# Every fourth weight piece: the low half by a ScalarE negation and an accumulating transfer instead of a VectorE subtraction

## The chip, the cores and the metric

The kernel runs on one core of one Trainium2 chip. The metric is the device time of one execution in microseconds. Before the change three runs took 945.02, 945.37 and 944.0 us, so the median is 945.02 us.

## The reference

Two layers of a hybrid encoder over 256 frames of width 2048. Each layer multiplies the frames by one wide input matrix, runs three groups of heads on the result (band attention, gated linear attention, attention into 256 memory frames), multiplies each group by a SiLU gate, and maps the concatenation back by an output matrix, with a residual and a layer norm. Cut to its matrix products:

```python
def hybrid_layer(x, mem, w_in, rel_table, gate_w, gate_b, gla_norm_g, w_mem_kv, w_out, ln_g, ln_b):
    h = x @ w_in                       # (256, 2048) @ (2048, 6672), split into a_q, a_k, a_v, a_z, b_*, m_*
    ...
    mkv = mem @ w_mem_kv               # (256, 2048) @ (2048, 1024)
    ...
    y = jnp.concatenate([y_a * jax.nn.silu(a_z), y_b * jax.nn.silu(b_z), y_m * jax.nn.silu(m_z)], axis=-1)
    out = y @ w_out                    # (256, 2048) @ (2048, 2048)
    return layer_norm(DEEPNORM_ALPHA * x + out, ln_g, ln_b)
```

All of it is float32. What takes the time are these products with weights: some 170 MB of weights are read once and each is used for 256 frames.

## The kernel before

**Products in two halves.** TensorE's fast 32-bit type (fp32r) holds fewer digits than float32. So each float32 operand is split into a high part (the value rounded to fp32r) and a low part (the value minus its high part, again fp32r), and a product is the sum of three: high by high, low by high, high by low. The helper `parts(hi, lo, src)` makes both parts: ScalarE copies `src` to `hi`, rounding it (L117), and VectorE subtracts `hi` from `src` into `lo` (L118).

**Pieces.** The weights come in pieces of 128 partitions x 1024 values (512 KB; those of the value projection 128 x 776, 388 KB). The helper `piece(src, n, kp)` (its transfer is at L140 or L138) takes three buffers, `raw`, `wh` and `wl`, from a pool `wp` with four buffers for each of the three names; SyncE's queue transfers the weights into `raw`, and `parts` makes `wh` and `wl`. TensorE then uses the piece at once: 16 matmuls in the groups that hold the weights still (`ws_half`), 12 in the groups that hold the frames still (`as_group`). A buffer comes free when its last reader is done. So the copy into `wh` of a piece waits for TensorE to be done with the piece four earlier, and its raw transfer waits until the subtraction of the piece four earlier has read `raw`.

**Order of the groups.** In each layer: memory values (`G_MV`, 8 pieces), memory keys (`G_MK`, 8), the gated heads' q and k (`G_BQK`, 8), values (32 of the narrower pieces, in four groups), q and k of the attention heads (32), memory q (8), four gate groups (32), and the output matrix (32, of which the last 8 each come as two transfers, because their source is a list). In layer 0 the first four pieces of all are made by another helper, `begin_pieces`. While a group runs, the heads' own small work (matmuls into tiles called `bk`) is mixed in between its pieces by `tick()`. From the last two gate groups to the end of the output matrix nothing is mixed in.

**What sets the order.** TensorE's and SyncE's instructions are issued in the order of the program. Those of VectorE, ScalarE and GpSimd are placed by a scheduler that simulates the kernel when it is built; `piece` runs at high priority. Each engine then works through its own list strictly in order, and an instruction that waits holds up all behind it.

**GpSimd** has little to do before the change: it starts the small transfers (gate weights, layer norm rows `ln_g` and `ln_b`, L707 and L708), clears a few tiles, and does six multiplications and additions of the layer norm between the layers (L515 and L516).

Lines of the kernel are given as in the program before the change; the change adds eight lines within and above `piece`, so that behind it L515 becomes L523.

## Time and profile before

| what | value |
|---|---|
| median of 3 runs | 945.02 us |
| the profiled execution's own time | 944.11 us |
| its span, first to last instruction | 942.3 us |
| time outside the span | 1.8 us |
| TensorE busy, share of the span | 98% |
| VectorE busy | 62% |
| ScalarE busy | 53% |
| GpSimd busy | 3% |
| mean granted TensorE clock | 0.994 |
| mean rate of transfers | 190 GB/s |

In the profile PE is TensorE's matmul side and PEld its weight loads, DVE is VectorE, ACT ScalarE, POOL GpSimd and SP SyncE. A busy TensorE is a modelled quantity, since matmuls overlap; whether it is truly at its pace is read from how evenly the pieces follow each other. A row of the timeline gives the start and the length in microseconds, the engine, the line, the operation with output and inputs, the shapes, and in brackets how long the engine sat idle before it and what ended that. "us to landing" is the time from the issue of a transfer until its data is there.

### The profile page before, as it was taken

Reading aid. Unit: us, or ns where it says so; the run is one execution under the profiler, and the core shown is the slowest. Engines: PE = TensorE matmul, PEld = TensorE weight load, DVE = VectorE, ACT = ScalarE, POOL = GpSimd, SP = SyncE. Lnnn points to the kernel's source line nnn. Section 1 sums busy time; section 2 is a strip of 40 time slices with the busy share of each in tenths; the row PEclk is TensorE's granted clock in tenths of the full one; section 3 lists DMA queues with packets and bytes.
Section 4 is the critical chain, followed back from the end, with each engine's and each line's share of the span. In section 5 each row is a group of like instructions: output and inputs, shape, how many; then the busy total and the mean of one; then the engine's idle time right before and its main releaser. Section 6 shows DMA issues by size and latency. Waiting matters only on the chain.

```text
span 942.3 us, 14178 instructions
## 1 busy us (share of the span) xinstructions
PE 927.4 (98%) x5506; PEld 812.6 (86%) x5506; DVE 584.6 (62%) x776; ACT 497.4 (53%) x711; POOL 30.4 (3%) x46
## 2 busy tenths in 40 slices
PE   7999999999999999999999999999999999999996
PEld 5889998898888888888878999889888888888884
DVE  5664487555555666555598545965545567566656
ACT  6554475366456665443465346644744576563340
POOL 1000000000000000000031000000000000010000
PEclk9999999999999999999999999999999999999997
DMA  8776865455555466866656465655555445676642
GB/s 267 252 273 177 298 196 167 148 186 167 191 160 162 158 188 194 255 190 193 222 187 227 142 207 177 201 161 176 156 192 173 158 156 159 200 244 205 200 134 89
DMA packets 61459, 178.75 MB, mean 190 GB/s; under 512 B 6824, under 2 KB 18376, under 8 KB 61136
## 3 DMA queue, kind: packets, MB, share of 16 engines
q1 hardware_dynamic: 59664, 173.56, 57.4%
q0 software_dynamic: 1728, 4.28, 1.9%
q8 instruction: 43, 0.70, 0.3%
q14 instruction: 24, 0.20, 0.1%
HBM read 175.69 MB, written 2.10 MB: 189 GB/s over the span
## 4 chain that ended last, share of the span: by engine, by line
PE 91%; DVE 3%; DMA 3%; issue 1%; ACT 1%; SPq 0%; DVEq 0%; ACTq 0%
PE acc L94 83%; PE bk L94 6%; DMA raw<-memT 1%; DVE wl L118 1%; DMA raw<-w 1%; PE bk L424 1%; PE bk L459 0%; DVE stats L499 0%; ACT x L117 0%; PE bk L483 0%; DVE res L518 0%; DVE res L586 0%; DVE res L498 0%; DVE res L519 0%; ACT wh L117 0%
## 5 line engine op out<-in xcount | busy, mean ns | idle before, releaser
L118 DVE TENSOR_TENSOR wl<-raw,wh 128x1024 fp32r<-128x1024 f32 (+3 forms) x325 | 378.0, 1166 | 273.7 <-ACT wh L117 268.2
L117 ACT CAST wh<-raw 128x1024 fp32r<-128x1024 f32 (+3 forms) x325 | 323.1, 995 | 348.8 <-PE acc L94 241.5
L94 PE MATMUL acc<-x,wh 128*128 128x512 f32 x1408 | 505.3, 401 | 0.0
L94 PE MATMUL acc<-x,wl 128*128 128x256 f32 x1408 | 394.7, 280 | 0.2 <-DVE wl L118 0.2
L94 PE MATMUL acc<-wh,x 128*128 128x512 f32 (+1 forms) x1120 | 322.7, 369 | 5.0 <-ACT wh L117 5.0
L94 PEld LDWEIGHTS acc<-x,wh 128*128 128x128 f32 x1408 | 264.3, 188 | 60.4 <-issue 0.3
L94 PEld LDWEIGHTS acc<-x,wl 128*128 128x128 f32 x1408 | 266.0, 189 | 0.9 <-DVE wl L118 0.5
L94 PEld LDWEIGHTS acc<-wh,x 128*128 128x128 f32 x1120 | 207.1, 189 | 31.2 <-ACT wh L117 6.4
L94 PE MATMUL acc<-wl,x 128*128 128x512 f32 (+1 forms) x560 | 206.3, 368 | 1.7 <-DVE wl L118 1.7
L94 PEld LDWEIGHTS acc<-wl,x 128*128 128x128 f32 x560 | 105.6, 189 | 14.9 <-DVE wl L118 2.9
L118 DVE TENSOR_TENSOR x<-raw,x 128x1024 fp32r<-128x1024 f32 (+2 forms) x16 | 15.3, 954 | 19.9 <-ACT x L117 19.9
L117 ACT CAST x<-raw 128x1024 fp32r<-128x1024 f32 (+2 forms) x16 | 13.4, 836 | 22.8 <-DMA raw<-memT 16.2
L416 ACT ACTIVATE sc<-sc,mx 128x128 f32<-128x128 f32 (+1 forms) x32 | 14.4, 450 | 17.8 <-DVE mx L414 17.7
L191 DVE SCALAR_TENSOR_TENSOR sc<-acc,sc 128x512 f32<-128x512 f32 x24 | 16.4, 681 | 0.0
L409 DVE SCALAR_TENSOR_TENSOR sc<-bk,bias 128x384 f32<-128x384 f32 x16 | 8.9, 554 | 10.3 <-PE bk L94 10.3
L190 ACT ACTIVATE sc<-acc 128x512 f32<-128x512 f32 x24 | 14.3, 595 | 0.0
L696 DVE TENSOR_TENSOR sc<-sc,yr 128x512 f32<-128x512 f32 x16 | 11.0, 690 | 5.2 <-ACT sc L692 5.2
L498 DVE SCALAR_TENSOR_TENSOR res<-res,acc 128x512 f32<-128x512 f32 x15 | 9.7, 684 | 7.2 <-PE acc L94 7.2
L94 PE MATMUL bk<-qk,qk 128*128 128x128 f32 (+1 forms) x64 | 13.1, 326 | 0.0
L94 PE MATMUL bk<-sc,asv 128*128 128x256 f32 (+1 forms) x64 | 13.0, 325 | 0.0
L692 ACT ACTIVATE sc<-sc 128x512 f32<-128x512 f32 x16 | 10.1, 629 | 4.6 <-DVE sc L191 4.5
L94 PEld LDWEIGHTS bk<-sc,asv 128*128 128x128 f32 x64 | 11.1, 188 | 1.5
(164 smaller groups left out, 497.6 us busy)
## 6 DMA issues: line engine op xcount, KB each, us to landing
raw<-w SPq DMA_DIRECT2D x236, 512.0 KB, 3.7
raw<-w SPq DMA_DIRECT2D x64, 388.0 KB, 3.1
raw<-w SPq DMA_DIRECT2D x39, 256.0 KB, 3.1
raw<-memT SPq DMA_DIRECT2D x6, 512.0 KB, 4.5
bias<-relw SPq DMA_DIRECT2D x16, 192.0 KB, 3.7
raw<-xT SPq DMA_DIRECT2D x4, 512.0 KB, 4.4
res<-xn SPq DMA_DIRECT2D x1, 2048.0 KB, 9.6
sc<-ln_g POOLq DMA_DIRECT2D x8, 256.0 KB, 5.3
```

Of the source, the lines that this page charges most:

```text
L94: pe.matmul(o, l, r, start=start, stop=stop, skip_group_check=True)
L117: act.copy(hi, src)
L118: dve.tensor_tensor(lo, src, hi.bitcast(F32), op=ALU.subtract)
L190: act.mul(dst, b, scale)
L191: dve.scalar_tensor_tensor(dst, a, scale, dst, op0=ALU.mult, op1=ALU.add)
L409: dve.scalar_tensor_tensor(s, pb[:, :384], SCALE, bias[h], op0=ALU.mult, op1=ALU.add)
L416: act.activation(s[:, own[t]], s[:, own[t]], AF.Exp, bias=mx[:, t:t + 1], accum_out=zs[:, t:t + 1])
L424: pe.transpose(pt[:, i * P:(i + 1) * P], s[:, i * P:(i + 1) * P], ident)
L498: dve.scalar_tensor_tensor(r, r, ALPHA, acc, op0=ALU.mult, op1=ALU.add)
L692: act.activation(sz, sz, AF.Silu)
L696: dve.tensor_tensor(sz, sz, yraw[i][:, j:j + 2], op=ALU.mult)
```

## The change

A counter counts the calls of `piece`. On every fourth call, unless the source is a list or the piece is one of the narrower ones (n = 388), the low part is made in another way. ScalarE copies `raw` to `hi`, as before, and then writes the negative of `raw`, rounded, into `lo`. Then GpSimd's queue issues a second transfer of the same weights from memory that adds them onto `lo`, which leaves `raw` minus its rounded value. VectorE has no part in such a piece.

```diff
     uid = [0]
+    pieces = [0]
...
             else:
                 sp.dma_start(raw.rearrange("p k n -> p (k n)"), src)
-            parts(hi, lo, raw)
+            pieces[0] += 1
+            if pieces[0] % 4 == 0 and not isinstance(src, list) and n != 388:
+
+                act.copy(hi, raw)
+                act.mul(lo, raw, -1.0)
+                pool.dma_start(lo.rearrange("p k n -> p (k n)"), src, accum_op=ALU.add)
+            else:
+                parts(hi, lo, raw)
         return hi, lo
```

This holds for 59 pieces, 29 in layer 0 and 30 in layer 1. As there are four buffers of each name, each changed piece uses the same `wl` buffer as the changed piece before it.

**ScalarE at a changed piece.** The first half of the last gate group, `G_MZ`, in layer 0; `raw`, `wh` and `wl` are the buffers of a piece and `sc` the gate's result. Before:

```order
L117 CAST wh_3491<-raw_3490 128x1024 [waits DMAHW6_49,PE_49,Activation_49]
L117 CAST wh_3513<-raw_3512 128x1024 [waits DMAHW7_49,PE_49,Activation_49]
L190 ACTIVATE sc_3434<-acc_3345 128x512 [waits PE_49]
L117 CAST wh_3540<-raw_3539 128x1024 [waits DMAHW0_49,DVE_49,PE_49]
L692 ACTIVATE sc_3434<-sc_3434 128x512 [waits DVE_49]
```

The same place now:

```order
L118 CAST wh_3512<-raw_3511 128x1024 [waits DMAHW6_49,PE_49,Activation_49]
L145 CAST wh_3534<-raw_3533 128x1024 [waits DMAHW7_49,PE_49,Activation_49]
L146 ACTIVATE wl_3535<-raw_3533 128x1024 [waits DMASW2_49,PE_49,Activation_49]
L198 ACTIVATE sc_3455<-acc_3365 128x512
L118 CAST wh_3562<-raw_3561 128x1024 [waits DMAHW0_49,DVE_49,PE_49]
L700 ACTIVATE sc_3455<-sc_3455 128x512 [waits DVE_49]
```

The negation stands directly behind the copy of its piece. TensorE's first matmul with the low part of that piece waited for DVE before, and now waits for a transfer from GpSimd's queue (DMASW):

```order
L94 MATMUL acc_3445<-x_568,wh_3513 128x512 [waits Activation_49]
L94 MATMUL acc_3445<-x_568,wl_3514 128x256 [waits DVE_49]
```

```order
L95 MATMUL acc_3466<-x_571,wh_3534 128x512 [waits Activation_49]
L95 MATMUL acc_3466<-x_571,wl_3535 128x256 [waits DMASW3_49,Activation_49]
```

The second matmul of the piece already needs the landed low part.

**GpSimd between the layers.** `res` is the residual that the layer norm scales, `sc` the rows `ln_g` and `ln_b`. Before:

```order
L708 DMA sc_4098<-ln_b 128x512 [waits DMASW5_49,DVE_49]
L515 ISA
L515 TENSOR_TENSOR res<-res,sc_3791 128x512 [waits DMAHW3_49,DMASW0_49,Activation_49]
L515 TENSOR_TENSOR res<-res,sc_3944 128x512 [waits DMASW2_49,Activation_49]
L516 TENSOR_TENSOR res<-res,sc_3792 128x512 [waits DMASW1_49,Pool_49]
L515 TENSOR_TENSOR res<-res,sc_4097 128x512 [waits DMASW4_49,Activation_49]
L516 TENSOR_TENSOR res<-res,sc_3945 128x512 [waits DMASW3_49,Pool_49]
L516 TENSOR_TENSOR res<-res,sc_4098 128x512 [waits DMASW5_49,Pool_49]
```

Now:

```order
L147 DMA wl_4391<-w 128x1024 [waits DMASW2_49,DMASW3_49,DVE_49,Activation_49]
L147 DMA wl_4474<-w 128x1024 [waits DMASW3_49,Activation_49]
L523 ISA
L523 TENSOR_TENSOR res<-res,sc_3816 128x512 [waits DMAHW3_49,Activation_49]
L523 TENSOR_TENSOR res<-res,sc_3971 128x512 [waits Activation_49]
L523 TENSOR_TENSOR res<-res,sc_4126 128x512 [waits Activation_49]
L524 TENSOR_TENSOR res<-res,sc_3817 128x512 [waits Pool_49]
L524 TENSOR_TENSOR res<-res,sc_3972 128x512 [waits Pool_49]
L524 TENSOR_TENSOR res<-res,sc_4127 128x512 [waits DMASW5_49,Pool_49]
L147 DMA wl_4577<-w 128x1024 [waits DMASW4_49,Activation_49]
```

The transfers for the fourth and eighth piece of layer 1 (`wl_4391`, `wl_4474`) stand ahead of the six layer norm operations, and that for the twelfth (`wl_4577`) behind them.

## The prediction

> **What bounds the kernel now.** I read the page first, then the chain of waits, the waits summed by pair, and the timeline of ScalarE.

> ```profile
> span 942.3 us, 14178 instructions
> PE 927.4 (98%) x5506; PEld 812.6 (86%) x5506; DVE 584.6 (62%) x776; ACT 497.4 (53%) x711; POOL 30.4 (3%) x46
> PE 91%; DVE 3%; DMA 3%; issue 1%; ACT 1%; SPq 0%; DVEq 0%; ACTq 0%
> L118 DVE TENSOR_TENSOR wl<-raw,wh 128x1024 fp32r<-128x1024 f32 (+3 forms) x325 | 378.0, 1166 | 273.7 <-ACT wh L117 268.2
> L117 ACT CAST wh<-raw 128x1024 fp32r<-128x1024 f32 (+3 forms) x325 | 323.1, 995 | 348.8 <-PE acc L94 241.5
> ...
> PEld acc L94 <- DVE wl L118: 3.4, 4, 1.6
> PE acc L94 <- DVE wl L118: 1.9, 3, 1.2
> ```

> TensorE is busy for 98% of the span and carries 91% of the chain. VectorE's subtraction (L118) is the largest group off TensorE, 378 us, but in the two last rows all waits of TensorE for it come to 3.4 + 1.9 us, start of the kernel included. ScalarE's copies (L117) sit idle for 241.5 us until TensorE gives a buffer back. So the preparation runs ahead of TensorE, held back only by the four buffers.

> How far ahead, the timeline of ScalarE shows in the last gate group of layer 0, where no head work is mixed in:

> ```profile
> 356.79 1.05 ACT L117 CAST wh<-raw 128x1024 fp32r<-128x1024 f32 x1 [1.72 <-PE acc L94]
> ...
> 365.11 1.05 ACT L117 CAST wh<-raw 128x1024 fp32r<-128x1024 f32 x1 [1.72 <-PE acc L94]
> 365.22 0.28 PE L94 MATMUL acc<-x,wl 128*128 128x256 f32 x1
> 367.89 1.05 ACT L117 CAST wh<-raw 128x1024 fp32r<-128x1024 f32 x1 [1.73 <-PE acc L94]
> ...
> 454.67 2.00 ACT L117 CAST wh<-raw 128x1024 fp32r<-128x1024 f32 x2
> ```

> The copy at 356.79 starts as TensorE returns the buffer. The next user of that buffer starts at 367.89, so four pieces take 11.10 us. TensorE needs the low part of the first at 365.22, its second matmul. That is 8.43 us after the copy starts.

> **What the change removes.** 59 subtractions of the 128x1024 form:

> ```profile
> L118 DVE TENSOR_TENSOR wl<-raw,wh 128x1024 fp32r<-128x1024 f32 x252 | 310.5, 1235 | 198.9 <-ACT wh L117 198.2
> 480.00:485.00 5.00, 3.83 (x17) 3.05 (x17) 4.96 (x9) 1.28 (x3) 0.00 (x0) 1.00 0.48 138
> 490.00:495.00 5.00, 4.84 (x30) 4.03 (x29) 5.00 (x3) 2.70 (x4) 5.00 (x4) 1.00 0.15 58
> ```

> 59 x 1.235 = 73 us of VectorE, nearly all under TensorE. The one place where VectorE holds TensorE up is the layer norm between the layers. The other two rows are windows there (length, then busy time of PE, PEld, DVE, ACT, POOL): VectorE is full and TensorE idles 1.17 + 0.16 = 1.33 us. That is all that the relief can give back.

> **What it adds on ScalarE.** 59 negations of 1024 values. A negation is not in this shape in the trace; the copy of the same shape takes 1.05 us and two copies back to back 2.00 us. 59 x 1.0 = 59 us makes ScalarE 556 us busy, 59%. It is covered by idle time such as the 1.72 us ahead of the copies above. Were that gone, the next piece's copy would start a microsecond late, still some 7 us ahead of its use.

> **What it adds on the path: the low part's latency.** Before, the low part was ready 1.05 + 1.24 us after the copy began. Now it is ready after copy and negation (2.0 us), a semaphore (0.1, my choice), and the transfer from issue to landing, which I call X. The margin for X is 8.43 - 2.0 = 6.4 us here. Each microsecond above it stalls TensorE at each such piece, and a stall isn't made up: the next changed piece uses the same `wl` buffer and starts its copy from the delayed end of this one.

> No accumulating transfer is in the trace, and no 512 KB from GpSimd's queue. The nearest rows (size, us to landing):

> ```profile
> raw<-w SPq DMA_DIRECT2D x236, 512.0 KB, 3.7
> raw<-w SPq DMA_DIRECT2D x39, 256.0 KB, 3.1
> raw<-w SPq DMA_DIRECT2D x2, 128.0 KB, 2.4
> ...
> ng<-norm_g POOLq DMA_DIRECT2D x1, 0.5 KB, 2.3
> ...
> sc<-ln_b POOLq DMA_DIRECT2D x1, 256.0 KB, 4.9
> ...
> sc<-ln_g POOLq DMA_DIRECT2D x1, 256.0 KB, 6.5
> ```

> The last three are single transfers of GpSimd's queue, at 216 us, at 387 us (little else moving) and at 379 us (amid weight loads). From below, X is SyncE's own 512 KB, 3.7 us, if GpSimd's queue and the addition cost nothing. From above, take GpSimd's slope, (4.9 - 2.3) us for 256 KB, and let the transfer move 1 MB, since an addition must also read what it adds to: 2.3 + 4 x 2.6 = 12.7 us. I choose between: 4.9 for 256 KB, plus 0.6 for going to 512 KB as on SyncE's queue (3.7 - 3.1), plus 1.7 for a second 512 KB at that queue's slope ((3.7 - 2.4) us for 384 KB): **X = 7.2 us**. The rows of `ln` transfers, from GpSimd's own queue, weigh most here, and 4.9 is the quieter of the two.

> [...]

> **The margins of all 59.** The same subtraction (first use of `wl` by TensorE, less the copy's start, less 2.0) over the 59 places falls into three classes. The tight ones:

> ```profile
> 24.76 1.05 ACT L117 CAST wh<-raw 128x1024 fp32r<-128x1024 f32 x1 [1.37 <-DMA raw<-w]
> ...
> 28.29 0.39 PE L94 MATMUL acc<-wl,x 128*128 128x512 f32 x1
> ...
> 56.56 1.05 ACT L117 CAST wh<-raw 128x1024 fp32r<-128x1024 f32 x1 [1.17 <-DMA raw<-w]
> ...
> 61.87 0.28 PE L94 MATMUL acc<-x,wl 128*128 128x256 f32 x1
> ...
> 469.37 1.05 ACT L117 CAST wh<-raw 128x1024 fp32r<-128x1024 f32 x1
> ...
> 474.55 0.39 PE L94 MATMUL acc<-wl,x 128*128 128x512 f32 x1
> ```

> Here the raw transfers come late, at the start of each layer, so the copy is not four pieces ahead. The margins are 1.5 us (first pair), 3.3 (second) and 3.2 (third). Three more lie in the same stretches, at 4.6, 5.3 and 5.9. With 7.2 + 0.1 these six cost 5.8 + 4.0 + 4.1 + 2.7 + 2.0 + 1.4 = 20 us.

> Twenty-three have 6.4 to 6.8 us: those of the last gate groups and the output matrix, where the rows of 356.79 and these stand for the rest, and a few among the heads.

> ```profile
> 411.51 1.05 ACT L117 CAST wh<-raw 128x1024 fp32r<-128x1024 f32 x1 [1.67 <-PE acc L94]
> ...
> 422.39 1.06 ACT L117 CAST wh<-raw 128x1024 fp32r<-128x1024 f32 x1 [1.67 <-PE acc L94]
> ```

> In the output matrix four pieces take 10.88 us and the first low part is used half a microsecond into its piece, so the margin is the same. At a mean of 6.55: 23 x 0.75 = 17 us.

> The other thirty lie among the heads, where `bk` matmuls stretch the pieces:

> ```profile
> raw<-w SPq DMA_DIRECT2D x35, 512.0 KB, 3.5
> ...
> 201.41 1.05 ACT L117 CAST wh<-raw 128x1024 fp32r<-128x1024 f32 x1
> ...
> 212.93 0.28 PE L94 MATMUL acc<-x,wl 128*128 128x256 f32 x1
> ...
> 344.96 1.05 ACT L117 CAST wh<-raw 128x1024 fp32r<-128x1024 f32 x1 [2.21 <-issue]
> ...
> 354.12 0.28 PE L94 MATMUL acc<-x,wl 128*128 128x256 f32 x1
> ```

> In the 114 us from 232 to 346 there are 35 pieces, 13.0 us for four. The widest margin (201.41) is 9.5, the narrowest (344.96) 7.1, their mean 8.1. At X = 7.2 only two are reached, 0.4 us.

> **GpSimd's queue.** The transfer for `wl_4577` now stands behind six layer norm operations:

> ```profile
> 486.65 3.50 POOL L515 TENSOR_TENSOR res<-res,sc 128x512 f32<-128x512 f32 x2 [98.55 <-ACT res L514]
> ...
> 494.04 4.52 POOL L516 TENSOR_TENSOR res<-res,sc 128x512 f32<-128x512 f32 x2
> ```

> They end at 498.56. In the trace TensorE wants that piece at 499.1, so without other delays 7 us would be lost. The two stalls just before it push TensorE back 5.5 us, but GpSimd only about 3, since the layer norm's ScalarE work stands behind the second changed piece: some 4 us remain. Elsewhere on this queue (layer norm rows, gate weights) what stands ahead is released before the negation is done.

> **Bandwidth.** The accumulating transfers read 31 MB more, a sixth of the 179 MB that move now, and as much again on chip. Weight loads in the middle of a layer have microseconds to spare, so I charge nothing beyond X; at the two starts they are late already, and the stalls above give them the time back.

> Sum, against the profiled execution: 944.1 + 20 + 17 + 0.4 + 4 = **986 us** (the median of the runs, 945.0, lies 0.9 above that execution).

> **Rivals.** *The addition costs far more* (transfers serialise, or get half the engines beside the weight loads; for it the 6.5 us row; against it the 4.9). At X = 9.5 the tight six cost 34, GpSimd's place 6, the twenty-three 23 x 3.05 = 70 and the thirty about 46: 1100 us. *The steady state hides it*: at X = 5.5 only five tight places (10 us) and GpSimd's place (3) are left, 957 us. For it: SyncE's 3.7 us with 1.7 for the second read. [...] *Not slower*: below X = 3.3 us at most 2 us are lost at the first piece and 1.33 us won between the layers, about 945 us. Against it: GpSimd's smallest transfer takes 2.3 us already. That the change doesn't do what it says would show as 59 missing subtractions still there; the order of instructions speaks against it.

> **How the numbers follow.** My forecast (X from 6 to 8.5 us) gets 0.5, the dear addition 0.27, the hidden one 0.16, not slower 0.07. The range, 950 to 1115 us, leaves out the last case and the upper half of the dear one. A measurement of this kernel tells about 0.2%, 1.9 us, from no change: faster 0.02, same 0.06, slower 0.92.

> **What would show it.** Right: PE waits for a transfer into `wl` at most of the output matrix's changed pieces and at few among the heads; the accumulating transfers land after about 7 us; ACT at 556 us and DVE at 512 us busy, both with more idle time. Wrong: landing under 5 us, or TensorE's lost time sitting at ScalarE's copies or raw transfers instead.

## The result, and the profile after

The changed kernel takes 1021.46 us (median of 4 runs, 1014.12 to 1028.41), against 944.51 us for the kernel before on the same chip: a ratio of 1.081, with a 95% interval of 1.074 to 1.089. It is slower by 77 us. The forecast was 986 us, slower, by stalls of TensorE at the changed pieces. The result lies inside the range, and the loss is nearly twice the one forecast.

The rows of the changed kernel's page that answer to those shown of before (this execution took 1028.41 us):

```profile
span 1026.5 us, 14366 instructions
PE 955.1 (93%) x5506; PEld 824.5 (80%) x5506; DVE 520.0 (51%) x717; ACT 551.7 (54%) x770; POOL 77.5 (8%) x105
...
q0 software_dynamic: 10224, 35.22, 18.4%
...
L95 PE MATMUL acc<-x,wl 128*128 128x256 f32 x1408 | 400.9, 285 | 28.8 <-DMA wl<-w 28.5
...
L95 PE MATMUL acc<-wl,x 128*128 128x512 f32 (+1 forms) x560 | 211.7, 378 | 26.5 <-DMA wl<-w 25.3
...
L146 ACT ACTIVATE wl<-raw 128x1024 fp32r<-128x1024 f32 x59 | 62.2, 1054 | 0.0
...
raw<-w SPq DMA_DIRECT2D x236, 512.0 KB, 4.3
wl<-w POOLq DMA_DIRECT2D x59, 512.0 KB, 7.4
```

The engines' totals came out near what was worked out ahead: ScalarE 552 us busy (556 forecast), VectorE 520 (512), the negation 1.05 us each (1.0), and the accumulating transfer lands 7.4 us after its issue in the median (7.2). The loss is on TensorE, and it has two parts. Its idle time, the span less PE's busy time, went from 14.9 to 71.4 us, so 56.5 us; the two matmul rows put 53.8 us of that down to transfers into `wl`, 33 waits. And its busy time grew by 27.7 us, from 927.4 to 955.1, with the same 5506 matmuls. The forecast has nothing of the second part.

The granted clock explains most of it. The view by windows of the changed kernel, cut at 3.41 us, the length of the shortest stretches at half clock in its trace, such as 67.33 to 70.74. A row has start and end, length, PE's busy time, granted clock, share of the transfer engines and GB/s:

```profile
26.37:29.78 3.41, 3.11 (x13) 1.00 0.82 256
29.78:33.19 3.41, 0.00 (x0) 1.00 0.96 225
33.19:36.61 3.42, 0.00 (x0) 0.50 1.02 299
36.61:40.02 3.41, 2.62 (x6) 0.50 0.68 276
40.02:43.43 3.41, 3.41 (x10) 0.50 0.00 0
43.43:46.85 3.42, 3.42 (x21) 1.00 0.67 155
63.91:67.33 3.42, 1.47 (x9) 1.00 1.01 390
67.33:70.74 3.41, 3.41 (x13) 0.50 0.85 257
661.25:664.66 3.41, 1.64 (x10) 1.00 0.87 298
664.66:668.07 3.41, 3.41 (x22) 1.00 0.22 87
...
sum 44.37, PE 37.99; mean PE 3.80
```

TensorE waits 7.8 us for the first changed piece, and from 33.19 to 43.43 us its clock is at one half: 10 matmuls fit in a full window there (13 in the one from 67.33), 21 or 22 at full clock. A window with 1.95 us of idleness was followed by half clock (63.91), one with 1.77 us was not (661.25). The last row is the sum over the ten such stretches ahead of the program's tail: 44.4 us long, 38.0 us of them busy. From the granted 0.50 I estimate that half of this, 19.0 us, would not be there at full clock; by the pace of the matmuls, whose pairs start 0.64 us apart at half clock (from 68.17) and 0.35 us apart behind it (from 71.09), it would be 17 us. In before there is no such stretch until the tail.

The other 8.7 us of added busy time stand nearly all at the same places. The first matmul with the low part of a piece of the output matrix in before, with the row ahead of it:

```profile
397.94 0.61 PE L94 MATMUL acc<-wh,x 128*128 128x512 f32 x2
398.39 0.39 PE L94 MATMUL acc<-wl,x 128*128 128x512 f32 x1
```

It starts before those ahead of it have ended (at 398.55), so only 0.23 us of its 0.39 are its own. The same matmul in the changed kernel (439.30, shown further below) stands behind a wait, overlaps nothing and lasts 0.47 us. Counted in this way, matmul by matmul, over the windows at full clock, the first matmuls with the low parts have 8.0 us more of their own than in before, at 38 pieces, in the median 0.24 us each. As the profile models the ends of matmuls, a wait that ended at full clock thus cost its length and some 0.24 us more here.

Where the idle time stands, piece by piece, in the prediction's own classes (TensorE's gap ahead of the first matmul with each low part, from its timeline):

| pieces | idle time forecast, us | measured, us |
|---|---|---|
| six tight ones at the layers' starts | 20 | 17.4 |
| `wl_4577`, behind the layer norm on GpSimd's queue | 4 | 3.3 |
| the twenty-three with margins of 6.4 to 6.8 us | 17 | 25.0 |
| all others (29 pieces) | 0.4 | 9.0 |
| sum | 41 | 54.6 |

The 20 changed pieces of the last two gate groups and the output matrix, which hold most of the third row, have 23.5 us of it all. The second row agrees by luck, as GpSimd's timeline at that place shows (the six operations of the layer norm, then the transfer for `wl_4577`):

```profile
533.19 4.13 POOL L523 TENSOR_TENSOR res<-res,sc 128x512 f32<-128x512 f32 x3
536.96 4.08 POOL L524 TENSOR_TENSOR res<-res,sc 128x512 f32<-128x512 f32 x3
545.10 0.89 POOL L147 DMA_DIRECT2D wl<-w  x1 [4.06 <-ACT wl L146]
```

The operations took 7.9 us, from 533.19 to 541.04, where they took 11.9 in before, and GpSimd then sat idle for 4.06 us until ScalarE's negation was done. So the layer norm did not hold this transfer at all. It landed late, after 10.5 us, the slowest of the 59, with three weight loads beside it, issued within 3.1 us of it, that took 6.2 to 7.7 us.

And one changed piece of the output matrix in the timeline of the changed kernel:

```profile
429.96 1.05 ACT L145 CAST wh<-raw 128x1024 fp32r<-128x1024 f32 x1 [6.62 <-PE acc L95]
430.91 1.05 ACT L146 ACTIVATE wl<-raw 128x1024 fp32r<-128x1024 f32 x1
431.99 8.76 SPq L141 DMA_DIRECT2D raw<-w  x4
432.27 0.86 POOL L147 DMA_DIRECT2D wl<-w  x1 [9.26 <-ACT wl L146]
...
439.30 0.47 PE L95 MATMUL acc<-wl,x 128*128 128x512 f32 x1 [0.56 <-DMA wl<-w]
```

The negation ends at 431.96, the transfer is issued at 432.27, and TensorE starts 7.03 us later, having idled 0.56 us. Less that, and less the 2.0 us of copy and negation, its lead was 439.30 - 429.96 - 0.56 - 2.0 = 6.8 us: the margin was right. Note the third row: the same negation releases the raw buffer, and SyncE's next weight load starts 0.28 us before the accumulating transfer. That comes back below.

### The profile page after: what moved, and what is told of

It reads as the page before. It is cut to its first block, busy times and chain, and to the rows that moved or that the text cites. A ratio compares the mean times of both kernels' runs of the same rounds, so it can differ in the third digit from the quotient of the medians.

```text
span 1026.5 us, 14366 instructions
## 1 busy us (share of the span) xinstructions
PE 955.1 (93%) x5506; PEld 824.5 (80%) x5506; DVE 520.0 (51%) x717; ACT 551.7 (54%) x770; POOL 77.5 (8%) x105
## 3 DMA queue, kind: packets, MB, share of 16 engines
q0 software_dynamic: 10224, 35.22, 18.4%
## 5 line engine op out<-in xcount | busy, mean ns | idle before, releaser
L95 PE MATMUL acc<-x,wh 128*128 128x512 f32 x1408 | 514.0, 406 | 0.0
L119 DVE TENSOR_TENSOR wl<-raw,wh 128x1024 fp32r<-128x1024 f32 (+3 forms) x266 | 308.8, 1162 | 279.5 <-ACT wh L118 278.5
L95 PE MATMUL acc<-x,wl 128*128 128x256 f32 x1408 | 400.9, 285 | 28.8 <-DMA wl<-w 28.5
L118 ACT CAST wh<-raw 128x1024 fp32r<-128x1024 f32 (+3 forms) x266 | 261.2, 983 | 245.1 <-PE acc L95 177.4
L95 PE MATMUL acc<-wh,x 128*128 128x512 f32 (+1 forms) x1120 | 329.1, 375 | 5.6 <-ACT wh L118 5.6
L95 PE MATMUL acc<-wl,x 128*128 128x512 f32 (+1 forms) x560 | 211.7, 378 | 26.5 <-DMA wl<-w 25.3
L145 ACT CAST wh<-raw 128x1024 fp32r<-128x1024 f32 x59 | 61.9, 1048 | 142.9 <-PE acc L95 97.2
L147 POOL DMA_DIRECT2D wl<-w x59 | 51.1, 865 | 804.1 <-ACT wl L146 647.7
L146 ACT ACTIVATE wl<-raw 128x1024 fp32r<-128x1024 f32 x59 | 62.2, 1054 | 0.0
L199 DVE SCALAR_TENSOR_TENSOR qk<-acc,qk 128x512 f32<-128x512 f32 x16 | 11.0, 690 | 36.9 <-ACT qk L198 36.9
L118 ACT CAST x<-raw 128x1024 fp32r<-128x1024 f32 (+2 forms) x16 | 13.3, 834 | 21.2 <-DMA raw<-memT 14.6
L506 DVE SCALAR_TENSOR_TENSOR res<-res,acc 128x512 f32<-128x512 f32 x15 | 9.7, 684 | 12.7 <-PE acc L95 12.7
## 6 DMA issues: line engine op xcount, KB each, us to landing
raw<-w SPq DMA_DIRECT2D x236, 512.0 KB, 4.3
wl<-w POOLq DMA_DIRECT2D x59, 512.0 KB, 7.4
raw<-w SPq DMA_DIRECT2D x39, 256.0 KB, 4.1
raw<-memT SPq DMA_DIRECT2D x6, 512.0 KB, 4.5
raw<-xT SPq DMA_DIRECT2D x4, 512.0 KB, 5.5
```

The source lines that it names most:

```text
L95: pe.matmul(o, l, r, start=start, stop=stop, skip_group_check=True)
L118: act.copy(hi, src)
L119: dve.tensor_tensor(lo, src, hi.bitcast(F32), op=ALU.subtract)
L145: act.copy(hi, raw)
L146: act.mul(lo, raw, -1.0)
L147: pool.dma_start(lo.rearrange("p k n -> p (k n)"), src, accum_op=ALU.add)
```

## The experiments

Three theories stood against each other first. LATENCY: the chain of copy, negation, issue and landing is longer than the lead that TensorE leaves it. BANDWIDTH: 59 more transfers of 512 KB slow all the loading. SCALARE: the second pass of ScalarE holds up the copies of other pieces.

**The negation without the transfer.** The line that issues the accumulating transfer is taken out:

```diff
                 act.mul(lo, raw, -1.0)
-                pool.dma_start(lo.rearrange("p k n -> p (k n)"), src, accum_op=ALU.add)
```

> The changed kernel without its 59 accumulating transfers: the low part of a changed piece is left as the negated high part, so the products miss the weights' low digits there. ScalarE's 59 negations stay and VectorE's 59 subtractions stay away. Three theories. LATENCY: a changed piece loses the time by which its low part lands after the margin of four buffers, and TensorE's clock halves for some microseconds after the longer stalls; then nothing is lost here: 943 to 947 us, granted clock 0.99. BANDWIDTH: the transfers' traffic delays the weight loads; also 943 to 947. SCALARE: the negations and their place in ScalarE's list hold up the next copies; then most of the 77 us stays, 980 to 1020.

Measured: 947.73 us, ratio 1.003 (1.002 to 1.004). ScalarE is as busy as in the changed kernel:

```profile
PE 927.0 (98%) x5506; PEld 811.7 (86%) x5506; DVE 520.2 (55%) x717; ACT 551.9 (58%) x770; POOL 29.6 (3%) x46
```

SCALARE is out as the main cause. The run is 2.7 us slower than the kernel before; 2.1 us of that show in its trace as two waits of `bk` matmuls for ScalarE (L423), which before doesn't have. The run also prices the other side of the change: with 59 subtractions gone from VectorE and nothing to wait for in their place, the kernel is not faster. VectorE's relief is worth nothing here.

**The transfer without a reader.** The kernel before, plus the same 59 transfers, each added onto the raw buffer once both of its readers are done, where nobody reads it again:

```diff
                 parts(hi, lo, raw)
+                pool.dma_start(raw.rearrange("p k n -> p (k n)"), src, accum_op=ALU.add)
```

> The kernel before (copy and subtraction for all pieces), with the same 59 accumulating transfers of the same weights added behind, onto the raw buffer, where nobody reads them; the negation is left out. The raw buffer comes free about 7 us later, which its lead of four pieces covers by some 3 us in the steady state, not at the layers' starts. LATENCY: 945 to 960 us. BANDWIDTH: the traffic of the changed kernel is all there, so 1000 to 1020. SCALARE: 945.

Measured: 956.02 us, ratio 1.012 (1.007 to 1.016).

```profile
span 951.3 us, 14305 instructions
...
q0 software_dynamic: 10224, 35.22, 21.3%
...
raw<-w SPq DMA_DIRECT2D x236, 512.0 KB, 4.5
raw<-w POOLq DMA_DIRECT2D x59, 512.0 KB, 5.5
```

BANDWIDTH is out as the main cause: the same bytes cost 11 us when TensorE doesn't wait for them. But they don't cost nothing, as the forecast had it: SyncE's own loads land in 4.5 us instead of 3.7. The 11 us need not be the price of the bytes alone, since the next load into a raw buffer now waits for the unread transfer to land: ScalarE's copies wait 127 us in all for weights here, 25 in the kernel before. How the 11 us are shared between the two no run shows. The transfers themselves land in 5.5 us, 1.9 sooner than in the changed kernel.

**A transfer without the addition.** The plain transfer overwrites the low part:

```diff
-                pool.dma_start(lo.rearrange("p k n -> p (k n)"), src, accum_op=ALU.add)
+                pool.dma_start(lo.rearrange("p k n -> p (k n)"), src)
```

> The changed kernel with the transfer as a plain one, without addition: the low part becomes the weights themselves, so the products are wrong by that. LATENCY with the split of the prediction (1.7 us of 7.2 for the second read): landing in about 5.7 us, 955 to 965 us. If the addition costs nothing and GpSimd's queue takes the time: landing in 7 us, 1010 to 1025. BANDWIDTH: half of the added traffic, about 980.

Measured: 966.18 us, ratio 1.022 (1.021 to 1.024).

```profile
span 964.0 us, 14366 instructions
...
q0 software_dynamic: 10224, 35.22, 10.6%
...
wl<-w POOLq DMA_DIRECT2D x59, 512.0 KB, 4.6
```

With 2.8 us less from issue to landing the loss falls from 77 to 21 us, through the same chain and with the same packets. The shares of q0 give the price of the addition on the transfer engines. The kernel before has this on its queue without the 59 transfers:

```profile
q0 software_dynamic: 1728, 4.28, 1.9%
```

That is 1.9% of 942.3, or 17.9 us. The 59 plain transfers take 10.6% of 964.0 less that, 84 us, or 1.43 us each on every one of the 16 engines; the accumulating ones 18.4% of 1026.5 less that, 171 us, or 2.90 us each. With the addition the packets took 2.03 times as long. That is not the time to landing: the same working gives 3.13 us for each of the unread transfers, which landed 1.9 us sooner. Whether the factor is a second read or the addition's own work no run here tells.

**Buffers of their own.** The changed pieces (and every second of those with a list as their source) get two of the four `wl` buffers for themselves, the others share the other two, and the negation comes ahead of the copy:

```diff
-            lo = wp.tile([P, kp, n], F32R, name=nm("wl"), tag="wl")
+            own = n != 388 and (pieces[0] + 1) % (2 if isinstance(src, list) else 4) == 0
+            lo = wp.tile([P, kp, n], F32R, name=nm("wl"), tag="wlx" if own else "wl", bufs=2)
...
-                act.copy(hi, raw)
                 act.mul(lo, raw, -1.0)
+                act.copy(hi, raw)
```

> The changed kernel with two of the four low part buffers kept for changed pieces and two for the others, and the negation ahead of the copy, so that the negation and the transfer need not wait for the changed piece four earlier. The margin grows by 4 to 5 us. LATENCY: stalls only at the layers' starts, 948 to 965 us. BANDWIDTH and SCALARE: the same traffic and the same ScalarE work, 1000 to 1020.

Measured: 983.79 us, ratio 1.043 (1.040 to 1.047), between the two expectations. The waits of TensorE:

```profile
PE acc L95 <- DMA wl<-w: 18.6, 6, 6.4
PE acc L95 <- DVE wl L119: 10.8, 7, 4.5
```

Waits for the transfer fall from 33 to 6. But the pieces with only two buffers now wait for VectorE, so this run is no clean test: it pays on one side what it saves on the other.

**Low parts last.** In each changed piece the matmuls on its high part all come first, so that the low part is needed some 1.9 us later; nothing else moves (the same edit stands in `as_group`):

```diff
-            for j in range(4):
-                for b in range(2):
...
+            for part in ((0, 1) if late else (2,)):
+                for j in range(4):
+                    for b in range(2):
+                        if part != 1:
+                            mm(acc[:, b].rearrange("p h t -> p (h t)"), wh[:, j, cs], both[:, j], pc == j == 0, False)
+                        if part != 0:
+                            mm(acc[:, b, 1], wl[:, j, cs], xh[:, j], False, pc == j == 3)
```

> The changed kernel, with one edit: of every fourth piece all matmuls on its high parts come first, and those on its low parts after them, so that the low parts are needed some 1.9 us later; the same matmuls, transfers and bytes. LATENCY (the chain cast, negation, issue, landing is longer than the lead that TensorE leaves it, and nothing else): of the idle time at the changed pieces in the changed kernel's trace (56 us more than before) about 13 us are left, with some three stretches of half clock behind them, so 955 to 970, most likely 962; TensorE's busy time falls from 955 to about 935. BANDWIDTH (59 more transfers of 512 KB slow all the loading): the load is the same, so over 1005. SCALARE (two passes of ScalarE per piece hold up the casts of the next pieces): the passes are the same, so over 1005.

Measured: 975.06 us, ratio 1.033 (1.031 to 1.035).

```profile
PE acc L95 <- DMA wl<-w: 11.6, 5, 5.2
```

The wait for the transfer falls from 53.8 to 11.6 us, as LATENCY had it, and 46 of the 77 us are gone with the same bytes and the same passes. The time is 13 us above the most likely figure and 5 above the range: landings grew to a median of 7.7 us, and four stretches of half clock are left (their busy time is 18.4 us, so they cost 9.2 by the same estimate).

**The two halves of the change apart.** One kernel leaves the first 24 pieces of each layer as they were, the other changes only those:

```diff
-            if pieces[0] % 4 == 0 and not isinstance(src, list) and n != 388:
+            if pieces[0] % 4 == 0 and (pieces[0] + 4) % 160 > 24 and not isinstance(src, list) and n != 388:
```

> The changed kernel without changed pieces among the first 24 pieces of each layer, where the lead was shortest in the trace of before: 48 or so transfers are left. LATENCY with the prediction's own terms: 20 us for the six tight pieces and 4 us for the piece behind the layer norm go, so about 962 of the 986 forecast stay, and of the 1021 measured 997. LATENCY as the changed kernel's trace shows it: 21 us of idle time go and with it some six stretches of half clock at 1.7 us each, so 980 to 993. BANDWIDTH: a fifth of the transfers goes, so a fifth of the 77 us: about 1006. What is left must stand at the pieces of the output matrix and the last gate.

> The other part of the change alone: only the 11 pieces among the first 24 of each layer are changed, and none behind them. The prediction's terms: 20 us for the six tight pieces and 4 for the piece behind the layer norm, 968. By the changed kernel's trace: 20.6 us of idle time there and some six stretches of half clock at 1.7 us each, 970 to 980. The two parts apart (this one, and the other part's 47 us above before) should add up to the 77 us of the whole within 8 us if a stall costs what it costs where it stands; a sum clearly under 77 would mean that the parts aggravate each other.

Measured: 990.76 us without the starts, ratio 1.050 (1.047 to 1.053); 976.08 us with the starts alone, ratio 1.033 (1.030 to 1.036). TensorE's largest wait in the first and in the second:

```profile
PE acc L95 <- DMA wl<-w: 32.3, 26, 3.0
```

```profile
PE acc L95 <- DMA wl<-w: 23.1, 8, 7.1
```

Against the kernel before on the same chip they lose 46.9 and 31.8 us, together 78.8, and the whole loses 77: the parts add up. The starts have few and long waits, the rest many and short ones, 1.2 us on average.

**Both edits at once**: no changed piece at the starts, and low parts last.

> Both edits at once: no changed piece among the first 24 of each layer, and of every fourth piece the matmuls on the low parts last; 48 accumulating transfers are left. LATENCY: of the waits for transfers in the trace with the low parts last (11.6 us), those at the starts go (11.3 of them) and perhaps 5 at the other long landings are left, with one stretch of half clock, and the load of 48 more transfers costs 48/59 of the 11 us that it cost when nothing waited for it: 953 to 962, most likely 957. BANDWIDTH or SCALARE: 48/59 of the 77 us stay, about 1007.

Measured: 951.8 us, ratio 1.009 (1.006 to 1.012).

```profile
PE acc L95 <- ACT wh L118: 5.2, 2, 4.8
PE acc L95 <- DMA wl<-w: 3.5, 2, 2.8
```

48 of the 59 transfers still run, and 7.6 us of loss are left (the time is just under the range expected), with 3.5 us of waits and no stretch of half clock ahead of the tail. This is the lowest of the kernels that use the transfers' result, and it is still above the kernel before.

**What halves the clock.** STALL: TensorE's own idleness does it. LOAD: it comes with the accumulating transfers. Two kernels tell it apart without any such transfer: the kernel before, with the subtraction of every sixth piece of the output matrix repeated eight (or six) more times, so that TensorE has to wait for VectorE there:

```diff
+            if pieces[0] % 6 == 0 and not isinstance(src, list) and kp == 2 and n == 512 and (pieces[0] + 4) % 160 > 24:
+                for _ in range(8):
+                    dve.tensor_tensor(lo, raw, hi.bitcast(F32), op=ALU.subtract)
```

> The kernel before, with the subtraction of every sixth piece of the output matrix written nine times over instead of once (eight places, same result, no accumulating transfer anywhere): VectorE holds the low parts back there, and TensorE stalls for 3 us or more at each place. STALL (TensorE's clock is halved for a stretch of 3.4 us or more by the stall itself, whatever caused it): in these stretches of the program the granted clock drops to 0.5 behind the stalls, as behind those of the changed kernel, and TensorE's busy time grows by 1.7 us or more a place, 8 to 25 us in all over the 928 of before; the time is 944 plus the stalls plus that. LOAD (the halved clock comes with the accumulating transfers, by their load on the memory or the chip's power): busy time stays at 928 within 3 us, and the time is 944 plus the stalls alone.

> As the kernel with the subtraction written nine times over, with seven times instead of nine, so that the stalls at the eight places are some 2.4 us shorter. STALL: behind stalls under about 1.8 us the clock stays at full speed, behind those over 3 us it is halved, so busy time grows by less than with nine (0 to 15 us). LOAD: busy time stays at 928 within 3 us in both.

Measured: 1029.08 us with eight (ratio 1.090, 1.088 to 1.092) and 1010.79 with six (1.071, 1.069 to 1.073). With eight, PE's row, its waits, the windows behind the first stall, and the sum over the eight stretches of half clock:

```profile
PE 946.2 (92%) x5506; PEld 824.3 (80%) x5506; DVE 658.9 (64%) x840; ACT 497.2 (48%) x711; POOL 30.4 (3%) x46
```

```profile
PE acc L95 <- DVE wl L146: 65.4, 8, 10.5
```

```profile
383.67:387.08 3.41, 0.00 (x0) 1.00 0.79 267
387.08:390.49 3.41, 0.00 (x0) 0.50 0.56 177
390.49:393.91 3.42, 1.44 (x3) 0.50 0.15 26
393.91:397.32 3.41, 3.41 (x9) 0.50 0.39 141
397.32:400.73 3.41, 3.41 (x16) 1.00 0.16 19
...
sum 75.09, PE 35.97; mean PE 4.50
```

Behind each of the eight stalls the granted clock fell to 0.50, with no accumulating transfer in the program. Busy time grows by 18.8 us over before, and half of the 35.97 busy at half clock is 18.0. STALL holds: a stall was enough, and LOAD was not needed. With six repeats the stalls came out longer than meant (4.5 to 8.0 us, 45.2 in all) and cost as much on the clock, 19.6 us of busy time: the surcharge did not follow the length of the stalls. The short stalls were not tested by these two, only by the windows of the changed kernel shown above.

**What the 7.4 us are made of.** The unread transfers landed in 5.5 us, those of the change in 7.4. The difference in the traces is the weight load that the negation releases at the same moment. A one-column addition on GpSimd, which reads the raw buffer and the landed low part, holds that load back until the landing; once with the accumulating and once with the plain transfer:

```diff
                 pool.dma_start(lo.rearrange("p k n -> p (k n)"), src, accum_op=ALU.add)
+                pool.tensor_tensor(small([P, 1], "late"), raw[:, 0, 0:1], lo[:, 0, 0:1].bitcast(F32), op=ALU.add)
```

> The changed kernel, with a one-column addition on GpSimd behind each accumulating transfer that reads the raw buffer and the landed low part, so that the raw buffer is released by the landing and not by the negation; the result is the same. In the changed kernel's trace the weight load into that buffer is issued 0.27 us before the accumulating transfer (median), released by the same negation, and the transfer lands after 7.4 us; in the run with unread transfers the next load comes 2 us or more behind, and they land after 5.5. BESIDE (the load that the same negation releases takes the transfer's share): landing falls to 5.3 to 6.0 us; by the prediction's margins the time at 5.5 is 957, and loads that come some 5 us later may cost at the layers' starts, so 955 to 978. OWN (adding into a low-part buffer takes that long by itself): landing stays at 7.2 or more and the time at 1010 or more.

> The same one-column addition behind a plain transfer in place of the accumulating one; the low parts of every fourth piece are wrong, since the weights replace the negated high part. Without it the plain transfer landed after 4.6 us. BESIDE: below 4.3 us, and the time below the 966 of the plain transfer, 950 to 965, unless the later loads cost it. OWN: 4.6 stays, and the time at 963 or more. The four landings (with and without the addition, with and without the load beside) give the price of each.

Measured: 997.86 us (ratio 1.056, 1.053 to 1.060) and 978.48 (1.035, 1.033 to 1.037). The issues of the first, and of the second:

```profile
wl<-w POOLq DMA_DIRECT2D x59, 512.0 KB, 5.4
```

```profile
wl<-w POOLq DMA_DIRECT2D x59, 512.0 KB, 3.8
```

| median from issue to landing, us | next load beside it | next load behind it |
|---|---|---|
| plain | 4.6 | 3.8 |
| accumulating | 7.4 | 5.4 |

BESIDE holds for the landings, both times. The addition costs 1.6 us by itself and 2.8 with a load beside it; the load costs 0.8 on the plain transfer and 2.0 on the accumulating one.

The times missed, by 20 us and by 13. The held loads are late now. The timeline of the first, at the piece next to the one shown of the changed kernel:

```profile
419.87 0.88 POOL L147 DMA_DIRECT2D wl<-w  x1 [5.91 <-ACT wl L146]
...
425.23 0.18 POOL L148 TENSOR_TENSOR late<-raw,wl 128x1 f32<-128x1 f32 x1 [4.47 <-DMA wl<-w]
425.43 2.94 SPq L141 DMA_DIRECT2D raw<-w  x4
...
429.16 1.05 ACT L145 CAST wh<-raw 128x1024 fp32r<-128x1024 f32 x1 [2.39 <-DMA raw<-w]
```

The next copy waits 2.39 us for its weights, and the lead is spent there. And at two places GpSimd started the layer norm's row transfers in one go behind the held step, beside which the accumulating transfer took 12.3 and 13.4 us. TensorE still waits 33.3 us for `wl`, at 10 places instead of 33. Shortening the landing by delaying the load moved the loss; it did not remove it.

## Why the prediction was right, and where it was off

*What bounds the kernel; what the relief is worth.* Right. Without any wait in place of the subtractions the time is 947.7, not below before; the bound of 1.33 us of gain was, if anything, generous.

*The negation is hidden.* Right to within 2.7 us: the same run keeps all 59.

*The path and its margins.* Right, and the centre of the case. Waits move as the margins say: 2.8 us less landing takes 56 of the 77 us away, 1.9 us more lead takes 46, and the pieces among the heads mostly don't wait. At the six tight places the sum (17.4 us for 20) is partly luck: landings took 7.3 to 9.4 us there, and the leads had grown by 0.5 to 3.3 us over those in before.

*GpSimd's queue.* Wrong, though 3.3 us were measured for 4. The prediction had the transfer for `wl_4577` wait behind the layer norm; GpSimd was done with the layer norm 4.06 us before the negation, and what was late was the landing, 10.5 us. What the queue did not cost, a slow landing did.

*X = 7.2 us.* The sum was right, 7.4 measured; its split was not. It was put together from 4.9 for 256 KB, 0.6 for the larger size and 1.7 for the second read. No run shows the second read that the last stands for: the pages count 35.22 MB on q0 with the addition and without it. What the runs show in its place is 1.6 us for the addition, with no load beside it. But a plain 512 KB from GpSimd's queue takes 3.8 us when no load starts beside it, not 5.5, and the 2.0 us in between belong to the load that the negation releases. Two errors of about the same size cancelled, so that 7.2 came near by luck. Why the 256 KB of an `ln` row took 4.9 us, more than 512 KB of weights, no run shows; such a row is one row of memory written to all 128 partitions, and so a poor likeness of a piece.

*The steps around X.* "A semaphore (0.1, my choice)" was too small. From the negation's end to the issue it is 0.29 us, from the landing to the matmul 0.14. The two and the 0.2 more of X bring a piece with 6.55 us of margin from 0.75 to 1.28 us late; the twenty-three would thus cost 29 us, and cost 25.0, where they were put at 17.

*One value for all landings.* X runs from 5.8 to 10.5 us in the trace, and its spread reaches the wide margins: the pieces forecast at 0.4 us cost 9.0, though on average their margin holds. A stall is the excess of a landing over its margin where there is one, and nothing gives back where the landing is early; a mean can't carry such a sum.

*Bandwidth.* "I charge nothing beyond X" failed. The unread transfers cost 11 us, though perhaps in part by holding the raw buffers.

*What the forecast lacked.* It priced a stall at its own length. The halved clock behind it adds 19.0 us by the estimate above, a third of the idle time again, and the matmuls that start anew behind a wait most of another 8.7 us. With the stalls at 54.6 instead of 41, these two make up the difference from 986 to this execution's 1028: 13 + 19 + 9 = 41 us, of 42.

Why the runs of the changed kernel spread over 14 us, when those of before spread over 1.4, stays open. That the stalls fall into other windows of the clock from run to run is at most a part of it: the runs of 1027.20 and 1014.12 us had nearly the same mean granted clock, 0.982 and 0.983. No run isolates it.

*The rivals.* The dear addition needed X = 9.5, the hidden one 5.5; both are refuted by 7.4, though the time came out between the forecast and the dear case, for reasons of its own.

## What to carry to other kernels

An engine that is 62% busy and whose results TensorE hardly waits for gives nothing when it is relieved. Moving work from it to a chain with a transfer in it costs the excess of that chain's length over the lead, at each place apart, so lay the landings' spread beside the margins, not their mean. On an engine that is 98% busy price a stall above its own length: here it cost about half as much again. And look at what the last reader of a buffer releases: the transfer that it lets loose runs beside the one that is now urgent.

## What was not expected of the hardware

**In these runs an accumulating transfer suffered more from its neighbour than a plain one**: the same load beside it added 2.0 us to its landing (5.4 to 7.4), and 0.8 to that of a plain one (3.8 to 4.6).
